# The state space kernels of eight channel groups on four column tiles of TensorE

## The chip, the cores and the metric

The kernel runs on one core of a Trainium2 chip. The metric is the device time of one execution in microseconds (us), taken as the median of several runs. Profiles come from one execution recorded by the hardware profiler. The engines are named as the profile names them: PE is TensorE (with PEld for its weight loads), ACT is ScalarE, DVE is VectorE, POOL is GpSimd, and SP is the engine whose queue issues most of the transfers.

## The reference: what is computed

One decoder block over 512 tokens and 16 meta tokens of width 1024, in float32: a half-weighted SwiGLU, then attention and a state space layer side by side, gated and merged, then a second half-weighted SwiGLU and a norm.

```python
h = h + 0.5 * swiglu(rmsnorm(h, ffn1_norm[i]), ffn1_w1[i], ffn1_w3[i], ffn1_w2[i])
hn = rmsnorm(h, mix_norm[i])
q, k, v, u, g_attn, g_ssm = jnp.split(hn @ w_in[i], SPLITS, axis=-1)
attn = sliding_window_attention(q, k, v, attn_sinks[i])
y = s5_ssm(u, ssm_a_re[i], ssm_a_im[i], ssm_log_step[i], ssm_b_re[i], ssm_b_im[i],
           ssm_c_re[i], ssm_c_im[i], ssm_d[i])
...
h = h + merged @ w_out[i]
h = h + 0.5 * swiglu(rmsnorm(h, ffn2_norm[i]), ffn2_w1[i], ffn2_w3[i], ffn2_w2[i])
return rmsnorm(h, final_norm)[:, N_META:]
```

The state space layer has 32 channel groups of 16 channels, each with 64 complex states. The kernel works on it in chunks of eight time steps. Within a chunk, the output of a group is its input times a small matrix that depends on the parameters alone: for each of the eight distances in time, a 16 by 16 block (input channel by output channel). The row of these blocks, 16 by 128 numbers for one group, is what the change is about. It is the product of a 128 by 16 matrix (the input matrix of the group, real and imaginary states below each other) and a 128 by 128 matrix (powers of the state's decay times the output matrix, for eight steps and 16 channels).

## The kernel before, in words

**The large products.** Nearly all of the time goes to products of weights with activations. Each float32 weight tile comes by an SP transfer into a tile `raw` (line 156). ACT rounds it to a high part `whi` (line 173), DVE forms the rest `wlo` (line 174), and PE multiplies high by high, high by low and low by high, all as float32r (line 238 for the first products of a SwiGLU, line 412 for its second ones, line 414 in the second SwiGLU). One output tile of 128 rows is a unit; in the first SwiGLU a unit of line 238 has 48 matmuls, since the 528 columns are taken as two halves of 264. Weights are prepared two units ahead of their use: while unit i is multiplied, the piece of unit i + 2 is prepared (`prep_piece`, called behind the unit's products in `step`), and three buffers of `whi` and `wlo` stand for it.

**The order of the work.** Instructions run on each engine in the order in which the program writes them (`manual_schedule`). The parameters of the state space layer are worked out beside the first SwiGLU, by a generator, `ssm_params`. In the loop over the units of the first SwiGLU (line 848), each unit from the fifth on takes one step of this generator, up to its next `yield`, and puts it between its matmuls, in the middle of the unit (the callables `mids`, cut in by `accumulate`). A step that holds matmuls thus interrupts a run of large matmuls on PE.

**The place of the change.** The last part of `ssm_params` (lines 636 to 673) handles the groups in four batches of eight. For a batch, POOL works out `Qt` (lines 639 to 642) and `Pb` (lines 644 to 648). Two steps later come the kernels. In one step, four matmuls (line 656) put the kernels of four groups side by side into one PSUM tile `psK`, 16 partitions by 512 columns, and ACT copies it to the tile `Kt` (line 658). In the next step the same follows for the other four groups, with another PSUM tile. Then POOL adds the direct term on `Kt` (line 663) and issues eight transfers that spread it over the matrix `Mt` (line 666), and two further steps transpose `Pb` on PE (four transposes each, line 671) with an ACT copy to `Wt` (line 672). `Mt`, `Qt` and `Wt` are read much later, in the mixing stage (lines 943, 992 and 993). The PSUM tiles of the generator come from a pool of four buffers of one bank each, `ps_ax`.

These matmuls are float32, not float32r. The profile records two LDWEIGHTS and two MATMULs for each of them: 64 of each for 32 matmuls. Their left operand has 16 columns, so only 16 columns of the array yield output.

Of the kernel before, what the change touches and what calls it, by code (L numbers as in the profile page):

```python
# [8 lines left out]
F32 = mybir.dt.float32  # L9
# [36 lines left out]
GB = 8  # L46
# [19 lines left out]
def hybrid_block_kernel(  # L66
# [47 lines left out]
    def bcol(b):  # L114
        return (b // 2) * HALF + (b % 2) * 128

# [1 line left out]
    ident = const.tile([128, 128], F32, name="ident")  # L118
    ones = const.tile([128, 128], F32, name="ones")
    gT = const.tile([128, 32], F32, name="gT")  # L120
# [3 lines left out]
    mhalf = const.tile([128, 6], F32, name="mhalf")  # L124
    st = const.tile([128, 6], F32, name="st")

# [1 line left out]
    raws = []  # L128
    pieces = []

# [68 lines left out]
            flush()  # L199

    def step2(ua, ub, mids=()):
        """Two units of which the last tile of operands comes late: it goes last in both."""
        a, b = ua[0](*take(), None), ub[0](*take(), None)
        next(a)
        for m in mids:
            m()
        prep_piece()
        next(b)
        for g in (a, b):
            for _ in g:  # L210
                pass
        ua[1]()
        prep_piece()
        ub[1]()
# [6 lines left out]
        return r  # L221

    def accumulate(seq, emit, mids):
        """One accumulation group; the callables in mids go out between its matmuls."""
        cuts = {len(seq) * (j + 1) // (len(mids) + 1): m for j, m in enumerate(mids)}
        for n, args in enumerate(seq):
            if n in cuts:
                cuts[n]()
            emit(*args, n == 0, n == len(seq) - 1)
# [24 lines left out]
        else:  # L254
            mm3([(ps, lambda r, k: real(r[:, k, :]))], hi, lo, rhi, rlo, nk, mids, k0)

# [1 line left out]
    def ffn_plan(w1, w3, w2, chunks, head=0, tail=False):  # L258
        f0 = 0
        for ci, n in enumerate(chunks):  # L260
# [39 lines left out]
        both(add_raw(ND, 256, wsrc(w_out[0], 0, ND, d * 128, 256)))  # L300
    ffn_plan(ffn2_w1[0], ffn2_w3[0], ffn2_w2[0], CHUNKS2, tail=True)

# [1 line left out]
    def new_hg(cols=COLS, p=hg_p):  # L304
        hi = p.tile([128, ND, cols], F32R, tag="hgh", name="hgh")
        lo = p.tile([128, ND, cols], F32R, tag="hgl", name="hgl")
# [40 lines left out]
        V.tensor_copy(st[:, 0:4], ps[:, 0:4])  # L347
        return st

# [1 line left out]
    def ffn_units(hg, hT, n528, mm_ps, g_p, t_p, chunks, last_hook=None, first_mm=None, tail=False):  # L351
        """The units of one half-residual SwiGLU, hT += 0.5 * its output; with tail, the last chunk's
        down projection is left out and its operands are returned."""
        w = HALF if n528 else 256
        units = []

# [92 lines left out]
                units.append(down(gs, n, d, last_hook if last else None))  # L449
        return units, gs  # L450

# [1 line left out]
    persist = ExitStack()  # L453
    tabs = ExitStack()
    tab = {}
# [16 lines left out]
    def ssm_params(ps_p):  # L472
# [111 lines left out]
        PE.transpose(ps[:16, 256:288], dn, ident[:NG, :NG])  # L584
        V.tensor_copy(T7.rearrange("p q g -> p (q g)"), ps[:, 0:224])
        V.tensor_copy(dT, ps[:16, 256:288])
        # the even groups' rows stay on the lower partitions, the odd ones' on the upper
        for i, (dst, q) in enumerate(((c8[:, 0, :], 2), (c8[:, 1, :], 3), (m8, 4))):
            v = T7[:, q, :].rearrange("p (j e) -> p j e", e=2)
            G.tensor_copy(dst[0:64], v[0:64, :, 0])  # L590
# [45 lines left out]
        for b in range(NB):  # L636
            gsl = slice(GB * b, GB * b + GB)
            tq = pp.tile([128, GB, T + 1, 16], F32, tag="s4", name="tq", bufs=2)
            G.tensor_tensor(out=Qt[:, gsl], in0=lam(LR, b, T + 1), in1=vec(A, 0, b, T + 1), op=ALU.mult)
            G.tensor_tensor(out=tq, in0=lam(LI, b, T + 1), in1=vec(A, 1, b, T + 1), op=ALU.mult)  # L640
            yield
            G.tensor_tensor(out=Qt[:, gsl], in0=Qt[:, gsl], in1=tq, op=ALU.add)
            Pb = pp.tile([128, GB, T, 16], F32, tag="s4", name="Pb", bufs=2)
            G.tensor_tensor(out=Pb, in0=lam(LR, b, T), in1=vec(BB, 0, b, T), op=ALU.mult)
            yield
            tq = pp.tile([128, GB, T, 16], F32, tag="s4", name="tq", bufs=2)
            G.tensor_tensor(out=tq, in0=lam(LI, b, T), in1=vec(BB, 1, b, T), op=ALU.mult)
            G.tensor_tensor(out=Pb, in0=Pb, in1=tq, op=ALU.add)
            yield
            yield  # L650
            Kt = pp.tile([16, GB, T, 16], F32, tag="s4", name="Kt", bufs=2)
            for h in range(2):
                ps = ps_p.tile([128, 512], F32, tag="ax", name="psK")
                for i in range(4):
                    g = GB * b + 4 * h + i
                    PE.matmul(out=ps[:16, 128 * i:128 * i + 128], lhsT=BB[:, 0, g, :],  # L656
                              rhs=Qt[:, g, 0:T, :].rearrange("p t c -> p (t c)"), start=True, stop=True)
                S.activation(out=Kt[:, 4 * h:4 * h + 4].rearrange("p g t c -> p (g t c)"), in_=ps[:16, :], func=AF.Copy)
                yield
            dg = pp.tile([16, GB, 16], F32, tag="dg", name="dg")  # L660
            G.tensor_tensor(out=dg, in0=ident[:16, 0:16].unsqueeze(1).to_broadcast([16, GB, 16]),
                            in1=dT[:, gsl].unsqueeze(2).to_broadcast([16, GB, 16]), op=ALU.mult)
            G.tensor_tensor(out=Kt[:, :, 0, :], in0=Kt[:, :, 0, :], in1=dg, op=ALU.add)
            for s in range(T):
                r0 = 16 * (T - 1 - s)
                G.dma_start(out=Mt[r0:r0 + 16, gsl, 16 * s:128],
                            in_=Kt[:, :, 0:T - s, :].rearrange("p g t c -> p g (t c)"))
            for h in range(2):
                ps = ps_p.tile([128, 512], F32, tag="ax", name="psW")
                for i in range(4):  # L670
                    PE.transpose(ps[:, 128 * i:128 * i + 128], Pb[:, 4 * h + i].rearrange("p t c -> p (t c)"), ident)
                S.activation(out=Wt[:, GB * b + 4 * h:GB * b + 4 * h + 4, :].rearrange("p g c -> p (g c)"), in_=ps, func=AF.Copy)
                yield
# [19 lines left out]
                n += w  # L693
            yield

# [1 line left out]
    G.memset(ones, 1.0)  # L697
    G.memset(ident, 0.0)
    G.affine_select(out=ident, in_=ident, compare_op=ALU.not_equal, fill=1.0, base=0, pattern=[[-1, 128]], channel_multiplier=1)
# [30 lines left out]
        S.dma_start(out=xm[h], in_=meta_tokens[8 * h:8 * h + 8, :])  # L730
    G.dma_start(out=srow, in_=attn_sinks)
    S.activation(out=rcol[:, 0:1], in_=mhalf[:, 0:1], func=AF.Silu)
    # the tensor engine's clock rises while the first loads are under way
    ps = ax_ps.tile([128, 512], F32, tag="ax", name="ps_w")
    for _ in range(WARM):
        PE.matmul(out=ps[:, 0:128], lhsT=ones, rhs=ones, start=True, stop=True)
# [22 lines left out]
        S.activation(out=hg[0][:, d, o], in_=hT[:, d, o], func=AF.Copy, scale=gT[:, d:d + 1])  # L759

    def x_in(h, d):
        """Block columns d of token half h: the transpose, then the two parts one and two blocks later."""
        if d < ND:
            x_t(h, d)
        if 0 <= d - 1 < ND:
            x_hi(h, d - 1)
        if 0 <= d - 2 < ND:
            x_lo(h, d - 2)
# [6 lines left out]
    firsts = []  # L775

    def first_mm(p, hi, lo, mids):
        """The first two units take the first half of the tokens first, while the second is brought in."""
        firsts.append((p, hi, lo))
        u = len(firsts) - 1  # L780
        for i, h in [(0, 0)] if u == 0 else [(1, 0), (0, 1), (1, 1)]:
# [82 lines left out]
    sf.close()  # L864
    hg = hg2

# [1 line left out]
    hd = tc.dram_tile([128, ND, COLS], F32, name="h_keep")  # L868
    G.dma_start(out=hd, in_=hT)
    sres.close()  # L870
# [24 lines left out]
    ud = tc.dram_tile([NB, 128, T, NCH], F32, name="u_steps")  # L895

    def ev_u(b):
        """Step-major u: [channel, (step, chunk)], the two chunks of meta tokens first; by way of DRAM
        it comes back as [(7 - step, channel of the group), (group, chunk)]."""
        def f(p):  # L900
            t = s_p.tile([128, T, NCH], F32, tag="uT", name="uT", bufs=2)

# [151 lines left out]
    tabs.close()  # L1054
    persist.close()

# [1 line left out]
    ps1.close()  # L1058
    ps3 = ExitStack()
    mm_ps = pool("ps_mm3", 3, space=PSUM, c=ps3)  # L1060
# [21 lines left out]
        G.tensor_copy(vr[m], vT[m][:, :, 256:264].unsqueeze(1).to_broadcast([128, 8, 2, 8]))  # L1082

    vmeta(0)
    # masks, with the sign that the negated scores need
    for t, m0, p0 in ((mA, 0, 16), (mC, 128, 0)):
        G.memset(t, 0.0)
        G.affine_select(out=t[:, p0:p0 + 128], in_=t[:, p0:p0 + 128], compare_op=ALU.is_gt, fill=1e30, base=0,
                        pattern=[[1, 128]], channel_multiplier=-1)
        G.affine_select(out=t[:, 144:272], in_=t[:, 144:272], compare_op=ALU.is_ge, fill=1e30, base=0,  # L1090
                        pattern=[[-1, 128]], channel_multiplier=1)
    # hm[p, h]: 1 where row p of the stacked meta probabilities belongs to head h
    V.tensor_reduce(out=hm, in_=ident.rearrange("p (l h k) -> p h l k", l=2, h=4), axis=mybir.AxisListType.XY, op=ALU.add)

    def ksplit(m):
# [73 lines left out]
        att[n] = (E, pm, [])  # L1169

    def s2(n, c, kb):
        """One block of keys: the probabilities' transpose."""
        E, _, tiles = att[n][:3]
        ps = pt_ps.tile([128, 512], F32, tag="pt", name="ps_t")
        for h in range(4):
            PE.transpose(ps[:, 128 * h:128 * h + 128], E[:, h, c:c + 128], ident)
        ph = a_p.tile([128, 512], F32R, tag="ph", name="ph", bufs=2)
        pl = a_p.tile([128, 512], F32R, tag="pl", name="pl", bufs=2)
        S.activation(out=ph, in_=ps, func=AF.Copy)
        V.tensor_tensor(out=pl, in0=ps, in1=fr(ph), op=ALU.subtract)  # L1180
        tiles.append((ph, pl, kb))
# [123 lines left out]

        step(*u, mids=[lambda fs=fs: [f() for f in fs] for fs in cuts], prep=False, hold=i < len(units) - 1)

# [1 line left out]
    at.close()  # L1309
    ps3.close()  # L1310
    kv.close()
# [46 lines left out]
            bcast_r(ax_ps, dgs[0], SEQ)  # L1358
    ps4.close()

    # the last chunk's down projection by halves of the tokens, each half's norm behind the products
    ps5 = ExitStack()
    mm_ps = pool("ps_mm5", 3, space=PSUM, c=ps5)
    z_ps = pool("ps_z", 2, space=PSUM, c=ps5)
# [112 lines left out]
```

## Time and profile before

| what | value |
|---|---|
| median of three runs | 1161.07 us (1159.37 to 1162.34) |
| span of the profiled execution, first to last instruction | 1160.7 us |
| granted TensorE clock of that execution, mean | 0.991 |
| PE busy | 1141.6 us, 98% of the span |
| PE weight loads busy | 1016.8 us, 88% |
| DVE / ACT / POOL busy | 632.1 / 410.4 / 361.5 us |
| first and last matmul of line 656 | 140.7 and 295.9 us from the span's start |

The profiled execution's own time is its span, 1160.7 us; the median of the runs is 0.4 us above it, which is what may lie around the span. A timeline row gives the start of a piece of work in us from the span's start, its length, the engine, the line, what is written from what, the shapes, and how many instructions were merged into the row. Matmuls are pipelined and the record of one is longer than the step from one to the next, so steps are read from starts, not from lengths.

### The profile page before, as it was taken

The numbers are of one execution on the slowest core, as the hardware profiler recorded it, in microseconds if no ns is written. First come the engines' busy times: TensorE is split into PE (matmuls) and PEld (weight loads), VectorE is DVE, ScalarE is ACT, GpSimd is POOL, SyncE is SP. The second block draws the span as 40 slices with busy tenths as digits, with TensorE's granted clock in tenths as the row PEclk, the third lists the DMA queues.
The fourth block names the chain that finished last, engine by engine and source line by source line (L and its number), as shares of the span: only waits on it lengthen the run. The fifth ranks groups of instructions, "written<-read, shape, count | busy, mean of one in ns | idle before, by whom it ended". The sixth has DMA issues, their size and how long they took to land.

```text
span 1160.7 us, 17253 instructions
## 1 busy us (share of the span) xinstructions
PE 1141.6 (98%) x7022; PEld 1016.8 (88%) x7022; DVE 632.1 (54%) x956; ACT 410.4 (35%) x719; POOL 361.5 (31%) x488
## 2 busy tenths in 40 slices
PE   9999999999999999999999999999999999999997
PEld 7999999999999999987778778878888888888887
DVE  5446653645444363767776777564544444444454
ACT  5322232232222242446565464353322222232234
POOL 1966662543685030425454331021000000000003
PEclk7999999999999999999999999999999999999999
DMA  5533233322423246121122222432333223323221
GB/s 158 115 96 109 73 92 94 91 84 83 110 74 101 69 144 191 48 73 60 51 73 73 73 68 79 145 109 73 108 109 110 73 82 103 112 86 117 84 73 73
DMA packets 105582, 108.42 MB, mean 93 GB/s; under 512 B 7504, under 2 KB 101968, under 8 KB 105376
## 3 DMA queue, kind: packets, MB, share of 16 engines
q1 hardware_dynamic: 103104, 100.74, 27.8%
q0 software_dynamic: 2352, 6.52, 2.2%
q8 instruction: 55, 0.90, 0.3%
q14 instruction: 23, 0.19, 0.1%
q10 hardware_dynamic: 48, 0.07, 0.0%
HBM read 100.80 MB, written 5.34 MB: 91 GB/s over the span
## 4 chain that ended last, share of the span: by engine, by line
PE 88%; DVE 4%; ACT 3%; POOL 2%; issue 2%; DMA 1%; POOLq 0%; DVEq 0%; SPq 0%; ACTq 0%
PE p L238 58%; PE p L412 11%; PE p L414 8%; PE p L798 2%; PE p L1372 1%; DMA hT<-h_keep 1%; ACT E L1157 1%; POOL m L1200 1%; POOL E L1168 1%; PE psK L656 1%; PE psY L992 1%; DVE wlo L174 1%; PE ps_x L744 1%; PE psY L993 1%; PE psS L943 1%
## 5 line engine op out<-in xcount | busy, mean ns | idle before, releaser
L238 PE MATMUL p<-hgh,whi 128*128 128x264 f32 (+1 forms) x1408 | 403.4, 333 | 0.1
L238 PE MATMUL p<-hgl,whi 128*128 128x264 f32 (+1 forms) x1408 | 402.4, 332 | 0.0
L238 PE MATMUL p<-hgh,wlo 128*128 128x264 f32 (+1 forms) x1408 | 400.9, 331 | 0.5 <-DVE wlo L174 0.5
L174 DVE TENSOR_TENSOR wlo<-raw,whi 128x1024 fp32r<-128x1024 f32 (+2 forms) x192 | 254.0, 1323 | 104.5 <-ACT whi L173 102.2
L238 PEld LDWEIGHTS p<-hgh,whi 128*128 128x128 f32 x1408 | 238.5, 188 | 26.0 <-issue 1.5
L238 PEld LDWEIGHTS p<-hgh,wlo 128*128 128x128 f32 x1408 | 238.2, 188 | 24.6 <-DVE wlo L174 1.0
L238 PEld LDWEIGHTS p<-hgl,whi 128*128 128x128 f32 x1408 | 238.4, 188 | 22.4
L173 ACT ACTIVATE whi<-raw 128x1024 fp32r<-128x1024 f32 (+2 forms) x192 | 187.5, 979 | 133.1 <-PE p L414 72.2
L1388 POOL TENSOR_TENSOR acc<-acc,zq 128x256 f32<-128x256 f32 x12 | 8.9, 738 | 349.8 <-ACT zq L1381 349.7
L384 ACT ACTIVATE t<-t 128x528 f32<-128x528 f32 (+1 forms) x44 | 28.1, 639 | 164.3 <-DVE t L383 164.3
L394 ACT ACTIVATE gh<-t 128x528 fp32r<-128x528 f32 (+1 forms) x44 | 28.1, 639 | 159.2 <-DVE t L393 159.2
L432 DVE SCALAR_TENSOR_TENSOR hT<-p,hT 128x528 f32<-128x528 f32 (+1 forms) x56 | 39.1, 698 | 82.8 <-PE p L414 52.2
L412 PE MATMUL p<-gh,whi 128*128 128x264 f32 x352 | 72.8, 288 | 0.7 <-DVE hT L432 0.5
L412 PE MATMUL p<-gl,whi 128*128 128x264 f32 x352 | 71.5, 284 | 0.0
L412 PE MATMUL p<-gh,wlo 128*128 128x264 f32 x352 | 71.4, 284 | 0.0
L383 DVE TENSOR_TENSOR t<-p,r_bc 128x528 f32<-128x528 f32 (+1 forms) x44 | 30.7, 698 | 70.4 <-PE p L238 67.3
L393 DVE TENSOR_TENSOR t<-p,t 128x528 f32<-128x528 f32 (+1 forms) x44 | 30.7, 698 | 63.8 <-PE p L238 63.5
L412 PEld LDWEIGHTS p<-gh,whi 128*128 128x128 f32 x352 | 54.4, 188 | 2.3 <-issue 1.2
L414 PE MATMUL p<-gh,whi 128*128 128x512 f32 x144 | 56.0, 389 | 0.0
L414 PE MATMUL p<-gl,whi 128*128 128x512 f32 x144 | 56.0, 389 | 0.0
L414 PE MATMUL p<-gh,wlo 128*128 128x512 f32 x144 | 56.0, 389 | 0.0
L412 PEld LDWEIGHTS p<-gl,whi 128*128 128x128 f32 x352 | 54.6, 188 | 0.0
(322 smaller groups left out, 1516.1 us busy)
## 6 DMA issues: line engine op xcount, KB each, us to landing
raw<-in_ffn_w_dram SPq DMA_DIRECT2D x42, 1024.0 KB, 5.4
raw<-in_ffn_w_dram SPq DMA_DIRECT2D x24, 768.0 KB, 4.3
raw<-in_w_in_dram SPq DMA_DIRECT2D x16, 1024.0 KB, 5.5
raw<-in_ffn_w_dram SPq DMA_DIRECT2D x12, 512.0 KB, 3.5
raw<-in_w_out_dram SPq DMA_DIRECT2D x4, 1024.0 KB, 8.7
h_keep<-hT POOLq DMA_DIRECT2D x1, 2112.0 KB, 7.3
raw<-in_ssm_glu_a_dram SPq DMA_DIRECT2D x4, 512.0 KB, 3.6
raw<-in_ssm_glu_b_dram SPq DMA_DIRECT2D x4, 512.0 KB, 4.6
```

The source lines that it names most:

```text
L173: S.activation(out=hi, in_=src, func=AF.Copy)
L174: V.tensor_tensor(out=lo, in0=src, in1=fr(hi), op=ALU.subtract)
L238: PE.matmul(out=o, lhsT=w[:, k0 + k, :], rhs=sl(r, k), start=start, stop=stop)
L383: V.tensor_tensor(out=t1, in0=cell[1], in1=rb(), op=ALU.mult)
L384: S.activation(out=t1, in_=t1, func=AF.Silu)
L393: V.tensor_tensor(out=t3, in0=cell[3], in1=cell["t1"], op=ALU.mult)
L394: S.activation(out=gh, in_=t3, func=AF.Copy)
L412: PE.matmul(out=p[:, h, :HALF], lhsT=wt[:, k, :], rhs=gs[k][c][:, h, :], start=start, stop=stop)
L414: PE.matmul(out=p, lhsT=wt[:, k, :], rhs=gs[k][c].rearrange("p h c -> p (h c)"), start=start, stop=stop)
L432: V.scalar_tensor_tensor(out=hv(hT, d), in0=cell["p"], scalar=0.5, in1=hv(hT, d), op0=ALU.mult, op1=ALU.add)
L656: PE.matmul(out=ps[:16, 128 * i:128 * i + 128], lhsT=BB[:, 0, g, :], rhs=Qt[:, g, 0:T, :].rearrange("p t c -> p (t c)"), start=True, stop= ...
L798: PE.matmul(out=p[:, h, :HALF], lhsT=w[:, k, :], rhs=r[:, k, h * HALF:(h + 1) * HALF], start=(n == 0), stop=(n == 3 * ND - 1))
```

## The change

For each batch of eight groups there is now one tile `psK` instead of two. The eight matmuls are written one behind the other, in two rounds of four. In a round, the four matmuls go to the four column tiles of the array, at columns 0, 32, 64 and 96 (`tile_position`), and so to partitions 0, 32, 64 and 96 of the PSUM tile; the second round takes the columns 128 to 255 of the PSUM tile. Column tile j holds the groups 2j and 2j + 1. ACT then makes four copies of 16 by 256 in place of two of 16 by 512, each from another quarter of the partitions to the same 16 partitions of `Kt`. The first two copies stand in the step of the eight matmuls, the other two in the next step, which has no matmul any more. The number of steps is the same. The rest of the file differs in comments and docstrings only; line numbers from 660 on rise by two.

```diff
             Kt = pp.tile([16, GB, T, 16], F32, tag="s4", name="Kt", bufs=2)
-            for h in range(2):
-                ps = ps_p.tile([128, 512], F32, tag="ax", name="psK")
-                for i in range(4):
-                    g = GB * b + 4 * h + i
-                    PE.matmul(out=ps[:16, 128 * i:128 * i + 128], lhsT=BB[:, 0, g, :],
-                              rhs=Qt[:, g, 0:T, :].rearrange("p t c -> p (t c)"), start=True, stop=True)
-                S.activation(out=Kt[:, 4 * h:4 * h + 4].rearrange("p g t c -> p (g t c)"), in_=ps[:16, :], func=AF.Copy)
-                yield
+            ps = ps_p.tile([128, 512], F32, tag="ax", name="psK")
+            for i in range(2):
+                for j in range(4):
+                    g = GB * b + 2 * j + i
+                    PE.matmul(out=ps[32 * j:32 * j + 16, 128 * i:128 * i + 128], lhsT=BB[:, 0, g, :],
+                              rhs=Qt[:, g, 0:T, :].rearrange("p t c -> p (t c)"), start=True, stop=True, tile_position=(0, 32 * j), skip_group_check=True)
+            for j in range(4):
+                S.activation(out=Kt[:, 2 * j:2 * j + 2].rearrange("p g t c -> p (g t c)"), in_=ps[32 * j:32 * j + 16, 0:256], func=AF.Copy)
+                if j % 2:
+                    yield
```

On PE, in the middle of the unit that takes the first of the two steps of the first batch, stand the following rows before the change (`p` is the unit's product, `hgh` and `hgl` the two parts of the activations):

```order
L238 MATMUL p<-hgl,whi 128x264 x2
L238 MATMUL p<-hgh,wlo 128x264 x2
L656 MATMUL psK<-Qt,BB 16x128 x4
L238 MATMUL p<-hgh,whi 128x264 x2
L238 MATMUL p<-hgl,whi 128x264 x2
```

At the same place after the change:

```order
L238 MATMUL p<-hgl,whi 128x264 x2
L238 MATMUL p<-hgh,wlo 128x264 x2
L656 MATMUL psK<-Qt,BB 16x128 x8
L238 MATMUL p<-hgh,whi 128x264 x2
L238 MATMUL p<-hgl,whi 128x264 x2
```

The eight matmuls of the batch now interrupt one unit; the middle of the next unit, where the other four stood, has none. The same holds for the other three batches.

On ACT, from the unit before the two steps to the one behind them, stand before the change (`t` and `gh` are tiles of the SwiGLU's evaluation):

```order
L384 ACTIVATE t_1610<-t_1610 128x528
L658 ACTIVATE Kt<-psK 16x512
L173 ACTIVATE whi<-raw 128x1024
L394 ACTIVATE gh<-t_1676 128x528
L658 ACTIVATE Kt<-psK 16x512
L173 ACTIVATE whi<-raw 128x1024
L384 ACTIVATE t_1741<-t_1741 128x528
```

And after it:

```order
L384 ACTIVATE t_1610<-t_1610 128x528
L659 ACTIVATE Kt<-psK 16x256 x2
L173 ACTIVATE whi<-raw 128x1024
L394 ACTIVATE gh<-t_1681 128x528
L659 ACTIVATE Kt<-psK 16x256 x2
L173 ACTIVATE whi<-raw 128x1024
L384 ACTIVATE t_1742<-t_1742 128x528
```

Each copy became two of half the columns, and nothing else moved on ACT.

## The prediction

> **What bounds the kernel now.** I read the page first: busy times and the chain of waits.
>
> ```profile
> span 1160.7 us, 17253 instructions
> PE 1141.6 (98%) x7022; PEld 1016.8 (88%) x7022; DVE 632.1 (54%) x956; ACT 410.4 (35%) x719; POOL 361.5 (31%) x488
> PE 88%; DVE 4%; ACT 3%; POOL 2%; issue 2%; DMA 1%; POOLq 0%; DVEq 0%; SPq 0%; ACTq 0%
> PE p L238 58%; PE p L412 11%; PE p L414 8%; PE p L798 2%; PE p L1372 1%; DMA hT<-h_keep 1%; ACT E L1157 1%; POOL m L1200 1%; POOL E L1168 1%; PE psK L656 1%; PE psY L992 1%; DVE wlo L174 1%; PE ps_x L744 1%; PE psY L993 1%; PE psS L943 1%
> ```
>
> PE is busy nearly throughout, and the chain that ends last runs over it; the kernels of the state space layer, line 656, are rounded to 1% of that chain, something like 10 us. A share of the whole program can hide a stage with another limit, so next comes the busy time in the stretch in which these matmuls lie (columns: window, its length, busy time and count on PE, PEld, DVE, ACT, POOL, then granted clock, DMA share, GB/s), and who made PE wait for weights.
>
> ```profile
> 140.00:310.00 170.00, 169.66 (x1379) 165.89 (x1378) 84.88 (x79) 47.03 (x64) 77.54 (x84) 1.00 0.31 88
> PE p L238 <- DVE wlo L174: 0.5, 1, 0.5
> ```
>
> In these 170 us PE is idle for 0.3 us, at the full clock, and every other engine is idle for at least half of the time. In the whole program PE waited once, for 0.5 us, for a weight part at line 238. So here a microsecond of PE is a microsecond of the kernel: what PE saves moves everything behind it forward.
>
> The third view is the chain in order of time, for the first and last of the eight bursts of line 656 (the eight rows are alike, 0.98 us each), and the tile's own rows.
>
> ```profile
> 140.77 0.98 PE psK L656 x8
> ...
> 295.18 0.98 PE psK L656 x8
> L656 PEld LDWEIGHTS psK<-Qt,BB x64: 92/97/97, 140.7 to 295.8; 128*16 128x16 f32 x64
> L656 PE MATMUL psK<-Qt,BB x64: 272/273/283, 140.7 to 295.9; 128*16 128x128 f32 x64
> ```
>
> A matmul is 273 ns from start to end, but a burst of eight instructions takes about 1 us: they overlap. What a burst really costs must be read from the timeline, around it.
>
> ```profile
> 139.63 0.41 PE L238 MATMUL p<-hgh,wlo 128*128 128x264 f32 x2
> ...
> 140.37 0.40 PE L238 MATMUL p<-hgh,wlo 128*128 128x264 f32 x2
> 140.70 1.05 PE L656 MATMUL psK<-Qt,BB 128*16 128x128 f32 x8
> 141.68 0.52 PE L238 MATMUL p<-hgh,whi 128*128 128x264 f32 x2
> 142.03 0.41 PE L238 MATMUL p<-hgl,whi 128*128 128x264 f32 x2
> ```
>
> Between 139.63 and 140.37 three pairs of large matmuls start: 0.74 / 3, some 0.245 us for a pair. From 140.37 to 142.03 are 1.66 us, in which two pairs go out (0.49 us). The burst costs the rest, **1.17 us**. Within it, the row's 1.05 us are seven steps and one whole matmul of 0.27 us, so one step is 0.78 / 7 = **0.11 us**. Eight steps are 0.88 us; the other **0.29 us** are a fixed cost of each burst. Is it the cost of any interruption? The transposes of line 671 answer that, full-width work cut into the same kind of run:
>
> ```profile
> 154.43 0.41 PE L238 MATMUL p<-hgh,wlo 128*128 128x264 f32 x2
> 154.67 0.60 PE L671 MATMUL psW<-ident,Pb 128*128 128x128 f32 x4
> 155.02 0.49 PE L238 MATMUL p<-hgh,whi 128*128 128x264 f32 x2
> 155.35 0.40 PE L238 MATMUL p<-hgl,whi 128*128 128x264 f32 x2
> ```
>
> From 154.43 to 155.35 are 0.92 us, less 0.49 for the two pairs: 0.43 us, which is four steps of 0.11 and nothing more. So the 0.29 us go with the narrow output: PE pays them for leaving the full array and coming back. The Trainium skill has this in "TensorEngine Tiling (Array Packing)", Key Properties: changing the tiling mode, not just the tile, drains the engine. The trace agrees, at 0.29 us for both changes.
>
> **The change part by part.** Before, a batch is two bursts, 2.34 us of PE; four batches are 9.4 us.
>
> *One interruption fewer per batch.* Eight matmuls now stand in one run between large ones, so the way out of the full array and back is paid once: 0.29 us less per batch, 1.2 us in all. This holds whatever else happens, unless changing the column tile costs something itself.
>
> *The 16 instructions on four column tiles.* No work in the trace of before goes to any column tile but the first, so it can't show whether tiles work side by side. The bounds are rows from above. At worst but for a penalty, the 16 go one behind the other, 16 x 0.11 = 1.76 us. At best, four tiles stream at once and the run is 4 x 0.11 = 0.44 us. Between the two decides the order of the two passes of a float32 matmul. The state space output later in the program, a narrow float32 product, shows it:
>
> ```profile
> 475.62 0.43 PE L992 MATMUL psY<-Mt,U 128*64 128x128 f32 x2
> 475.89 0.38 PE L993 MATMUL psY<-Qt,X 128*64 128x128 f32 x2
> 476.11 0.38 PE L992 MATMUL psY<-Mt,U 128*64 128x128 f32 x2
> ```
>
> The program writes one matmul of line 992, then one of line 993, and so on; PE gets each as two instructions in a row. So in the changed run the order is tile 0 twice, tile 1 twice, tile 2 twice. The two passes of one matmul use one tile and one output and can't go together. If PE starts instructions in order, the first pass on tile 1 can go beside the second pass on tile 0, but not sooner. Then the run is one step for the first pass, seven steps in which a second pass and the next matmul's first pass share the array, and one step for the last: 9 x 0.11 = 0.99 us. I take this value, between the two bounds, because of the rows of lines 992 and 993: tiles overlap, and the order that these rows show limits it to pairs. With the fixed 0.29 us a batch costs 1.28 us in place of 2.34: 1.06 us less, **4.2 us** in four batches.
>
> On the order, the Trainium skill says in "TensorE: Matmul & The Clock Gate", Part 3, that matmuls keep program order in start and in end. By this rule pairs are the most that can overlap, and the sum stays at 4.2 us; no row here shows it for several tiles.
>
> *ACT.* Half-size copies from PSUM are in the trace, of the same number of columns:
>
> ```profile
> L658 ACT ACTIVATE Kt<-psK 16x512 f32<-16x512 f32 x8 | 4.7, 589 | 28.2 <-PE psK L656 28.2
> L1113 ACT ACTIVATE VB<-ps_v 128x256 fp32r<-128x256 f32 x4 | 1.5, 379 | 0.1
>   POOL Kt L663: 81.9, 4
> L666 POOL DMA_DIRECT2D Mt<-Kt x32: 522/531/643, 150.3 to 301.4; - x32
> ```
>
> Two copies at 0.38 us take 0.76 in place of 0.59: 0.17 us more in each step, 1.4 us over the eight. In the first step of a batch they also start about 0.1 us later, since the run (1.28) is longer than a burst (1.17). Queued behind them on ACT is `whi` of line 173, then DVE's `wlo`, for a weight that PE uses two units on; a unit is 48 large matmuls, nearly 6 us. A delay of 0.3 us has that cover and costs nothing; bare, it would be 0.3 us at most for each of four units, 1.2 us. In the second step ACT no longer waits for PE at all, so its work there comes earlier. The copies end earlier for POOL too, which waited 81.9 us for them in four times, some 20 us each (the third row). Its eight transfers per batch keep their order on POOL's queue and are not short of time: the last is issued at 301.4 us (the fourth row), and `Mt`, which they fill, is first read at 475.62 us (the row of line 992). One PSUM tile fewer per batch leaves the pool's other uses as free as they were. All this at zero.
>
> The sum against the profiled span: 1160.7 - 4.2 = 1156.5 us; the median of the runs lies 0.4 above the span, so 1161.07 - 4.2 = **1156.9 us**, 0.36% less. What is late next is PE itself, with the large matmuls.
>
> **The rivals.**
>
> *No overlap.* The 16 instructions take their 1.76 us whatever the tile, 2.05 us per batch; only the saved interruption is left: 4 x 0.29 = 1.2 us, 1159.9 us. For it: float32 passes already take twice the steps per column of the float32r ones (128 columns in 0.11 us against 264 in 0.12), so something on the way in could be full. Against: with 16 of 128 columns in use, the array has the room.
>
> *Full overlap.* The passes of a matmul are issued, but tiles run ahead of each other, and four stream at once: 0.29 + 0.44 = 0.73 us per batch, 1.61 saved, 6.4 us in all, 1154.7 us. Against it: the pairs in the rows of line 992 and 993 come strictly in program order. The Trainium skill speaks for it in the same Part 3, with 2.38 times the speed for three column tiles; an estimate from 2.38 / 3 on four tiles would give 16 x 0.11 / 3.2 + 0.29 = 0.84 us and 6.0 us saved.
>
> *Changing the tile costs.* Seven of the 16 instructions go to another column tile than the one before. If each such change empties the array, or its weight load can't be hidden, the run gets longer than two bursts. The gain of 0.29 us is gone at 0.29 / 7 = 0.04 us per change; that is the point from which this rival makes the kernel slower. Prices from rows: a bare weight load, 0.097 us, added to the 2.05 us of the case without overlap gives 2.05 + 0.68 = 2.73 us against 2.34, 1.6 us slower; an emptied array, 0.273 - 0.11 = 0.16 us, gives 2.05 + 1.14 = 3.2 us, 0.85 more per batch, **3.4 us slower, 1164.5 us**; the whole 0.29 us of a mode change at each gives 7 us, 1168.1 us. For it: a change of mode is shown to cost that. Against: in the burst of before, weight loads of 0.097 us are wholly hidden in steps of 0.11, though all go to the same tile. The Trainium skill says, in that Part 3, that a weight load overlaps a running matmul only when the row group differs; the 0.11 us step, with one row group throughout, already speaks against taking this strictly.
>
> **How the numbers follow.** Pairs overlap (1156.9 us) 0.45; no overlap (1159.9) 0.25; full overlap (1154.7) 0.18; a tile change that costs (1162.6 to 1168.1) 0.12. About 0.3%, 3.5 us, is what a measurement of this kernel can tell from no change. The likeliest case lies 0.7 us beyond it, and the three runs spread over 3 us, so I count 0.32 of its 0.45 as faster; with full overlap that is 0.49. The rest of it, no overlap, and the cheap end of the tile change make 0.43 for within 0.3%; 0.08 is left for slower. The range takes in the first three cases with a microsecond around them, 1153.9 to 1161.0 us; left out are the costly tile change and the edges, somewhat under 0.2.
>
> **What the profile after would show.** Four bursts of line 656 with 16 instructions each, not eight with eight. Read as above, from the last large pair before a burst to the second after it, less 0.49 us: 1.28 us if pairs overlap, 2.05 if nothing does, 0.73 for full overlap, 2.7 or more if changing the tile costs. Within a burst, starts would come in pairs of nearly the same time, 0.11 us apart, in the first case, evenly 0.11 us apart in the second, in fours in the third. The middle of the following unit shows no interruption. ACT's copies should be near 0.38 us, eight per half. I would be wrong in the step "the gain passes through" if the burst shrinks as told but PE waits longer for `wlo` at line 238 or for `gh` at line 412 behind it.

## The result, and the profile after

The changed kernel takes 1155.44 us (median of five runs, 1154.81 to 1156.95), the kernel before 1162.07 us (median of five runs, the three of the table ahead of the prediction among them). The two medians are 6.6 us apart; the recorded ratio is 0.9949, with a 95% interval of 0.9936 to 0.9961, which is 5.9 us less, between 4.5 and 7.4, and so holds the 6.6 too. The forecast was 4.2 us less. It has the right sign and lies a little below this interval. The time itself, 1155.44, lies in the range, but that range was drawn wide enough for three different mechanisms, so it doesn't tell which of them is at work.

The page of the kernel after, the lines that were shown of before:

```profile
span 1154.1 us, 17264 instructions
PE 1135.5 (98%) x7022; PEld 1012.4 (88%) x7022; DVE 634.9 (55%) x956; ACT 411.6 (36%) x727; POOL 359.0 (31%) x488
PE 87%; DVE 4%; ACT 3%; POOL 2%; issue 2%; DMA 1%; SPq 0%; POOLq 0%; DVEq 0%; ACTq 0%
```

The stretch of the kernels, and the wait for weights at line 238:

```profile
140.00:310.00 170.00, 169.66 (x1430) 167.89 (x1430) 90.08 (x81) 49.41 (x73) 84.81 (x109) 1.00 0.32 95
```

```profile
PE p L238 <- DVE wlo L174: 0.2, 1, 0.2
```

PE does as many matmuls as before (7022) in 6 us less busy time, and is as full in the stretch as it was (idle 0.3 us of 170): more of its work fits into the same time, 1430 matmuls in place of 1379. No wait took the place of what went. Next, the timeline around the first batch, to be read as before the change:

```profile
140.58 0.40 PE L238 MATMUL p<-hgh,wlo 128*128 128x264 f32 x2
140.91 0.63 PE L656 MATMUL psK<-Qt,BB 128*16 128x128 f32 x16
141.47 0.51 PE L238 MATMUL p<-hgh,whi 128*128 128x264 f32 x2
141.82 0.41 PE L238 MATMUL p<-hgl,whi 128*128 128x264 f32 x2
```

From 140.58 to 141.82 are 1.24 us, less 0.49 for two pairs: **0.75 us** for a batch. Two bursts took 2.34. All four batches are alike, so 4 x 1.59 = 6.4 us went here, and the span fell by 1160.7 - 1154.1 = 6.6 us, at the same mean granted clock of 0.991. Nearly all of the gain is in this stage. How the 16 instructions share their 0.63 us is seen by ending the window a little later each time:

```profile
140.91 0.30 PE L656 MATMUL psK<-Qt,BB 128*16 128x128 f32 x4
140.91 0.41 PE L656 MATMUL psK<-Qt,BB 128*16 128x128 f32 x8
140.91 0.52 PE L656 MATMUL psK<-Qt,BB 128*16 128x128 f32 x12
```

The first four are done after 0.30 us, and one alone takes 0.28: they start within 0.02 us. Each further 0.11 us brings four more. Four steps, not nine: this is the rival "full overlap".

### The profile page after: what moved, and what is told of

It is laid out like the page before. It is cut to its first block, busy times and chain, and to the rows that moved or that the text cites. A ratio compares the mean times of both kernels' runs of the same rounds, so it can differ in the third digit from the quotient of the medians.

```text
span 1154.1 us, 17264 instructions
## 1 busy us (share of the span) xinstructions
PE 1135.5 (98%) x7022; PEld 1012.4 (88%) x7022; DVE 634.9 (55%) x956; ACT 411.6 (36%) x727; POOL 359.0 (31%) x488
## 4 chain that ended last, share of the span: by engine, by line
PE 87%; DVE 4%; ACT 3%; POOL 2%; issue 2%; DMA 1%; SPq 0%; POOLq 0%; DVEq 0%; ACTq 0%
PE p L238 58%; PE p L412 11%; PE p L414 8%; PE p L800 2%; ACT E L1159 1%; PE p L1374 1%; DMA hT<-h_keep 1%; POOL m L1202 1%; POOL E L1170 1%; DVE wlo L174 1%; PE psY L994 1%; PE psY L995 1%; PE psS L945 1%; PE ps_t L1178 1%; ACT whi L173 1%
## 5 line engine op out<-in xcount | busy, mean ns | idle before, releaser
L385 DVE TENSOR_TENSOR t<-t,r_bc 128x528 f32<-128x528 f32 (+1 forms) x44 | 37.2, 845 | 32.4 <-ACT t L384 32.4
```

What stands on the lines that cost most here:

```text
L385: V.tensor_tensor(out=t1, in0=t1, in1=rb(), op=ALU.mult)
```

## The experiments

Each kernel's batch is read off the timeline in the same way: from the last pair of large matmuls ahead of the run to the second pair behind it, less 0.49 us. The first batch is shown; in the chain of waits the four batches of a kernel have the same length. "Instruction" stands for one pass of a float32 matmul, with its own weight load; a matmul has two. The two kernels under "How far ahead" and the one under "The fixed cost" were executed once each, so only their batches are read and not their times.

**Theory and rivals after the result.** Four column tiles work at once, and the run takes as many steps of 0.11 us as the busiest tile has instructions, plus 0.29 us for leaving the full array and coming back. The rivals: the gain is that of the saved interruption or of the work that moves with it; or tiles do share the array, but PE starts instructions strictly in the order in which they reach it, and in the change the passes of a round's four matmuls happen to reach it interleaved (first pass of all four, then second pass of all four).

**One run on one tile.** All eight matmuls in one step, on the first column tile.

```diff
+            pk = []
             for h in range(2):
                 ps = ps_p.tile([128, 512], F32, tag="ax", name="psK")
+                pk.append(ps)
                 for i in range(4):
...
+            for h in range(2):
-                S.activation(out=Kt[...], in_=ps[:16, :], func=AF.Copy)
+                S.activation(out=Kt[...], in_=pk[h][:16, :], func=AF.Copy)
                 yield
```

> All eight matmuls of a batch stand in one step, as in the change, but all on the first column tile and in two PSUM tiles, with the two copies of before. Theory (four column tiles work at once, and the saved interruption is a side gain): 16 steps of 0.11 us and 0.29 us fixed, 2.05 us per batch in place of 2.34, so 1.2 us less than before, 0.1%. Rival (the gain is in the saved interruption, or in ACT's and POOL's work that moves with it): about 6 us less than before, as in the change.

The timeline of this kernel:

```profile
137.02 0.40 PE L238 MATMUL p<-hgh,wlo 128*128 128x264 f32 x2
137.36 1.92 PE L658 MATMUL psK<-Qt,BB 128*16 128x128 f32 x16
139.56 0.41 PE L238 MATMUL p<-hgl,whi 128*128 128x264 f32 x2
```

2.54 - 0.49 = 2.05 us per batch, 1.2 us less than before in four. The time is 0.9977 of before (0.9965 to 0.999), 1.2 to 4.1 us less. The interval's middle is above what the batches give; where the rest would be is not settled, but the 5.9 us of the change are outside it. The interruption is a minor part.

**Four tiles, two runs per batch.** The same number of interruptions as before.

```diff
-                for i in range(4):
-                    g = GB * b + 4 * h + i
-                    PE.matmul(out=ps[:16, 128 * i:128 * i + 128], ...)
-                S.activation(out=Kt[:, 4 * h:4 * h + 4]..., in_=ps[:16, :], func=AF.Copy)
+                for j in range(4):
+                    g = GB * b + 4 * h + j
+                    PE.matmul(out=ps[32 * j:32 * j + 16, 0:128], ..., tile_position=(0, 32 * j), skip_group_check=True)
+                for j in range(4):
+                    S.activation(out=Kt[:, 4 * h + j]..., in_=ps[32 * j:32 * j + 16, 0:128], func=AF.Copy)
                 yield
```

> Four column tiles, but four matmuls per step as before, so eight bursts of eight instructions, and one copy of 16 by 128 per group. Theory: two steps of 0.11 us and 0.29 us fixed, 0.51 us per burst in place of 1.17, so 5.3 us less than before. Rival (the saved interruption makes the gain): no change against before.

```profile
140.52 0.40 PE L238 MATMUL p<-hgh,wlo 128*128 128x264 f32 x2
140.86 0.41 PE L656 MATMUL psK<-Qt,BB 128*16 128x128 f32 x8
141.55 0.40 PE L238 MATMUL p<-hgl,whi 128*128 128x264 f32 x2
```

1.03 - 0.49 = 0.54 us per burst against 1.17, so 5.0 us in eight; the time is 0.9942 of before (0.9919 to 0.9965). The tiles alone make most of the gain.

**Two tiles.** The change on the columns 0 and 32 only.

```diff
-            for i in range(2):
-                for j in range(4):
-                    g = GB * b + 2 * j + i
+            for i in range(4):
+                for j in range(2):
+                    g = GB * b + 4 * j + i
...
-            for j in range(4):
-                S.activation(out=Kt[:, 2 * j:2 * j + 2]..., in_=ps[32 * j:32 * j + 16, 0:256], func=AF.Copy)
-                if j % 2:
-                    yield
+            for j in range(2):
+                S.activation(out=Kt[:, 4 * j:4 * j + 4]..., in_=ps[32 * j:32 * j + 16, :], func=AF.Copy)
+                yield
```

> As the change, but on two column tiles, at columns 0 and 32, with four matmuls for each and two copies of 16 by 512. Theory: eight steps of 0.11 us with two starts each and 0.29 us fixed, 1.17 us per batch, 4.7 us less than before. Rival (in order, passes of a matmul one behind the other): the first start alone, then pairs, nine steps, 1.28 us per batch, 4.2 us less than before.

```profile
137.24 0.40 PE L238 MATMUL p<-hgh,wlo 128*128 128x264 f32 x2
137.58 1.05 PE L656 MATMUL psK<-Qt,BB 128*16 128x128 f32 x16
138.91 0.41 PE L238 MATMUL p<-hgl,whi 128*128 128x264 f32 x2
```

16 instructions in the 1.05 us that eight took on one tile; 1.67 - 0.49 = 1.18 us per batch, eight steps and not nine. The time, 0.9945 of before (0.9924 to 0.9966), doesn't tell 4.7 us from 4.2; the batch does.

**Tile by tile.** Does PE start in order, with the passes interleaved, or does each tile go its own way? The order of writing tells.

```diff
-            for i in range(2):
-                for j in range(4):
+            for j in range(4):
+                for i in range(2):
                     g = GB * b + 2 * j + i
+                    m = 16 + 4 * i + j
-                    PE.matmul(out=ps[32 * j:32 * j + 16, 128 * i:128 * i + 128], lhsT=BB[:, 0, g, :], ...)
+                    PE.matmul(out=ps[32 * j:32 * j + m, 128 * i:128 * i + 128],
+                              lhsT=BB.rearrange("p a g c -> p (a g c)")[:, 16 * g:16 * g + m], ...)
```

> As the change, but the eight matmuls are written tile by tile: both matmuls of the first tile, then both of the second, and so on, so that four instructions for one tile stand behind each other. The left operands are 16 to 23 columns wide (the added output rows are read by nobody), so that each record tells its matmul. Theory (tiles run on their own, an instruction waits only for its own tile): starts still come in fours, of four different tiles, four steps of 0.11 us, 0.75 us per batch, and the time of the change, 6.4 us less than before. Rival (PE starts instructions in the order written, and in the change the two passes of the four matmuls of a round were interleaved on their way to it): a tile's first pass can start only beside the last pass of the tile before, so 13 steps, 1.72 us per batch, 2.5 us less than before.

The timeline, the first four by themselves and then all 16:

```profile
140.92 0.40 PE L238 MATMUL p<-hgh,wlo 128*128 128x264 f32 x2
141.25 0.33 PE L657 MATMUL psK<-Qt,BB 128*16 128x128 f32 x4
141.25 0.65 PE L657 MATMUL psK<-Qt,BB 128*16 128x128 f32 x16
142.18 0.40 PE L238 MATMUL p<-hgl,whi 128*128 128x264 f32 x2
```

The same first four, by their shapes (128*16 is an operand of 16 columns, and so the first tile's):

```profile
L657 PE MATMUL psK<-Qt,BB x4: 283/284/286, 141.3 to 141.3; 128*16 128x128 f32 x1, 128*17 128x128 f32 x1, 128*18 128x128 f32 x1, 128*19 128x128 f32 x1
```

The first four to start are one each of the widths 16, 17, 18 and 19, the four tiles, though three more instructions of the same tile are written between any two of them. An instruction overtakes those written ahead of it when they are another tile's. So the order of writing, which the description of the kernel before gives as the order on each engine, is not the order of starts on PE across column tiles. 1.26 - 0.49 = 0.77 us per batch, and 0.9959 of before (0.9944 to 0.9973), 3.1 to 6.5 us less: the theory's 6.4 lies in it, the rival's 2.5 doesn't. In-order start is out.

One more thing is in these rows. The first four take 0.33 us here and 0.30 in the change, one alone 0.284: three starts in 0.045 us against three in 0.017, some 14 ns against 6. Four instructions stand from one tile's first to the next's here, two in the change. This fits a PE that hands them out in the order written, some 3 to 4 ns each, to tiles that then work through their own; two differences of a few nanoseconds don't show it yet.

**How far ahead.** If so, how many instructions does a tile take ahead, before those behind them in the program have to wait? Two tiles, written tile by tile, with 16 and with eight instructions of the first tile ahead of the second's. The first edit is shown against the kernel of two tiles (its operand widths, changed as in the run before, are left out), the second against the first.

```diff
-            for i in range(4):
-                for j in range(2):
+            for j in range(2):
+                for i in [*range(4), *range(4)]:
```

> Two column tiles, written tile by tile, and each matmul made twice (the second time onto the same output), so that 16 instructions for the first tile stand ahead of the first one for the second tile; operands 16 to 23 columns wide as labels. Theory (PE hands instructions out in order, about 3.3 ns each, and each tile works through its own): the second tile starts 16 x 3.3 = 53 ns after the first, 16 steps of 0.11 us with two starts each, 2.05 us per batch. Rival (PE sees only a few instructions ahead, enough for the four of the tile-by-tile run but not more): the second tile starts only when some 12 of the first tile's instructions are gone, 12 x 0.11 = 1.3 us later, and the batch takes about 3.4 us.

The timeline of the first batch:

```profile
136.19 0.40 PE L238 MATMUL p<-hgh,wlo 128*128 128x264 f32 x2
136.53 3.25 PE L657 MATMUL psK<-Qt,BB 128*16 128x128 f32 x32
140.06 0.41 PE L238 MATMUL p<-hgl,whi 128*128 128x264 f32 x2
```

What of line 657 had started before 137.84 and before 137.86 us (the second tile's operands are 20 columns wide and more; a row lists its four commonest shapes):

```profile
L657 PE MATMUL psK<-Qt,BB x12: 272/272/283, 136.5 to 137.7; 128*16 128x128 f32 x4, 128*17 128x128 f32 x4, 128*18 128x128 f32 x2, 128*19 128x128 f32 x2
...
L657 PE MATMUL psK<-Qt,BB x14: 272/273/287, 136.5 to 137.9; 128*16 128x128 f32 x4, 128*17 128x128 f32 x4, 128*18 128x128 f32 x3, 128*19 128x128 f32 x2
```

Here the theory as I had put it falls, and the rival's number holds: 3.87 - 0.49 = 3.38 us per batch. Before 137.84 us twelve instructions of the first tile have started and nothing else. Two more follow at once: the thirteenth of the first tile (the third of width 18) and one of none of the four widths listed, which hold 13 of the 14; its width is 20, so it is the second tile's first. This would follow if a tile takes four ahead, the running one among them, and the fifth, with all behind it in the program, waits. A look-ahead that all tiles share doesn't give it: in the tile-by-tile run twelve instructions stood ahead of the fourth tile's first, and it started within 0.05 us. The same with eight ahead:

```diff
-                for i in [*range(4), *range(4)]:
+                for i in range(4):
```

> Two column tiles, written tile by tile, each matmul made once, so that eight instructions for the first tile stand ahead of the second tile's first. Theory (a tile takes four instructions ahead, the one that runs among them, and holds up those behind it in the program beyond that): the second tile starts with the fifth instruction of the first, 4 x 0.11 = 0.45 us after its start; 12 steps of 0.11 us and 0.29 us fixed, 1.6 us per batch. Rival (the second tile comes at once when its instructions are few enough, and the 16 of the run before were too many for one common queue): both tiles start within 0.03 us, 1.18 us per batch.

```profile
140.46 0.40 PE L238 MATMUL p<-hgh,wlo 128*128 128x264 f32 x2
140.80 1.50 PE L657 MATMUL psK<-Qt,BB 128*16 128x128 f32 x16
142.58 0.41 PE L238 MATMUL p<-hgl,whi 128*128 128x264 f32 x2
```

What had started before 141.24 and before 141.26 us:

```profile
L657 PE MATMUL psK<-Qt,BB x4: 272/272/283, 140.8 to 141.1; 128*16 128x128 f32 x2, 128*17 128x128 f32 x2
...
L657 PE MATMUL psK<-Qt,BB x6: 272/273/287, 140.8 to 141.2; 128*16 128x128 f32 x2, 128*17 128x128 f32 x2, 128*18 128x128 f32 x1, 128*20 128x128 f32 x1
```

Up to 141.24 us four of the first tile have started; the next two, by 141.26, are its fifth (width 18) and the second tile's first (width 20), some 0.45 us after 140.80. The batch takes 2.12 - 0.49 = 1.63 us, 12 steps. Four ahead was the number before the run, and it holds. In the tile-by-tile run four was just what each tile got, which is why it lost nothing.

**The fixed cost.** One run on one tile, with an operand as wide as the array.

```diff
-                    PE.matmul(out=ps[:16, 128 * i:128 * i + 128], lhsT=BB[:, 0, g, :],
+                    PE.matmul(out=ps[:, 128 * i:128 * i + 128], lhsT=BB.rearrange("p a g c -> p (a g c)")[:, 16 * g:16 * g + 128],
```

> The run of eight matmuls on one tile, with a left operand of 128 columns in place of 16 (the operands of the groups behind it; the added output rows are read by nobody), so that the array need not leave its full width. Theory (the fixed 0.29 us are the way from the full array to a column tile and back): 16 steps of 0.11 us and nothing fixed, 1.79 us per batch. Rival (the fixed cost goes with float32 between float32r, or with the run itself): 2.05 us per batch as with 16 columns.

```profile
137.50 0.40 PE L238 MATMUL p<-hgh,wlo 128*128 128x264 f32 x2
137.74 1.95 PE L658 MATMUL psK<-Qt,BB 128*128 128x128 f32 x16
139.76 0.40 PE L238 MATMUL p<-hgl,whi 128*128 128x264 f32 x2
```

2.26 - 0.49 = 1.77 us, against 2.05 with 16 columns: 0.28 of the 0.29 us go with the narrow operand, not with the float32 or the interruption. "TensorEngine Tiling (Array Packing)" in the Trainium skill, Key Properties, has a drain at a change of tiling mode; if that is the cost, these two runs give its price. That PE drains is not seen in a trace by itself.

**ACT's copies twice.** The change, each copy made two times.

```diff
             for j in range(4):
-                S.activation(out=Kt[:, 2 * j:2 * j + 2]..., in_=ps[32 * j:32 * j + 16, 0:256], func=AF.Copy)
+                for _ in range(2):
+                    S.activation(out=Kt[:, 2 * j:2 * j + 2]..., in_=ps[32 * j:32 * j + 16, 0:256], func=AF.Copy)
```

> The change, with each of ACT's copies made twice (same source, same place), 0.38 us more for each, 1.5 us of ACT more per batch, 6 us in all. Theory (ACT's copies lie beside PE's work and cost nothing): the time of the change. Rival (weights are held up behind the copies): up to 6 us more than the change.

The copies' row, of the change and then of this kernel:

```profile
L659 ACT ACTIVATE Kt<-psK x16: 373/377/381, 141.7 to 288.1; 16x256 f32<-16x256 f32 x16
```

```profile
L660 ACT ACTIVATE Kt<-psK x32: 372/376/380, 141.3 to 288.5; 16x256 f32<-16x256 f32 x32
```

16 copies more of 0.376 us, 6.0 us of ACT, and the time is 1156.25 us beside 1156.65 us of the change, run again on the same chip: 0.9941 of before (0.9925 to 0.9958) against 0.9936 (0.9918 to 0.9954). The rival's 6 us would have brought it back to about the time of before; ACT's part is off the path.

> The change itself, beside the next three on the same chip: 0.76 us per batch in place of 2.35, about 6.4 us less than before.

That second measurement of the change, 0.9936, agrees with the first.

**The outputs too.** What eight groups gain in the kernels, the state space outputs should gain on two tiles of 64 columns. Here too each tile gets four instructions in a row, the number that it takes ahead.

```diff
-        for h in range(2):
-            ps = ax_ps.tile([128, 512], F32, tag="ax", name="psY")
-            for i in range(4):
+        ps = ax_ps.tile([128, 512], F32, tag="ax", name="psY")
+        for i in range(4):
+            for h in range(2):
                 g = GB * b + 4 * h + i
-                o = ps[:64, 128 * i:128 * i + 128]
+                o = ps[64 * h:64 * h + 64, 128 * i:128 * i + 128]
-                PE.matmul(out=o, lhsT=u[:, 4 * h + i, 2:NCH], rhs=Mt[:, g, :], start=True, stop=False)
+                PE.matmul(out=o, lhsT=u[:, 4 * h + i, 2:NCH], rhs=Mt[:, g, :], start=True, stop=False,
+                          tile_position=(0, 64 * h), skip_group_check=True)
...
+                          tile_position=(0, 64 * h), skip_group_check=True)
-            S.activation(out=y[:, :, 4 * h:4 * h + 4, :]..., in_=ps[:64, :]..., func=AF.Gelu_apprx_tanh)
+        for h in range(2):
+            S.activation(out=y[:, :, 4 * h:4 * h + 4, :]..., in_=ps[64 * h:64 * h + 64, :]..., func=AF.Gelu_apprx_tanh)
```

> The change, and the state space outputs in the same manner: their matmuls yield 64 rows, and those of the upper four groups of a batch go to the column tile at 64, so that a batch has one PSUM tile psY in place of two, with two copies from its two halves. Theory (two tiles of 64 columns work at once just as four of 32): 16 steps of 0.11 us in place of 32 per batch, 1.75 us less in each of four batches, 7 us less than the change. Rival (matmuls that add onto an open output, or 64 columns wide, don't share the array, or the later start of the first copy makes PE wait): no change against the change.

The first batch's outputs, from the large pair ahead to the second pair behind, in the change:

```profile
469.12 0.40 PE L238 MATMUL p<-hgh,wlo 128*128 128x264 f32 x2
469.46 0.43 PE L994 MATMUL psY<-Mt,U 128*64 128x128 f32 x2
...
473.45 0.41 PE L238 MATMUL p<-hgl,whi 128*128 128x264 f32 x2
```

And in this kernel:

```profile
469.19 0.40 PE L238 MATMUL p<-hgh,wlo 128*128 128x264 f32 x2
469.52 0.45 PE L994 MATMUL psY<-Mt,U 128*64 128x128 f32 x4
...
471.81 0.41 PE L238 MATMUL p<-hgl,whi 128*128 128x264 f32 x2
```

4.33 - 0.49 = 3.84 us became 2.62 - 0.49 = 2.13 us: 1.71 less per batch, 6.8 us in four. The time is 1150.12 us, 0.989 of before (0.9874 to 0.9905), beside 0.9936 of the change. This version beats both kernels, by some 12 us and some 6.

## Why the prediction was right in direction and short in size

*PE bounds the stretch, so what PE saves moves the end.* Right: 6.4 us less in the four batches, 6.6 us less in the span, and PE's wait for `wlo` at line 238 went from 0.5 to 0.2 us.

*The cost of a burst, 1.17 us, with 0.29 us fixed.* Right in size: 0.28 us is what separates 16 columns from the full width in the runs on one tile, and in the batches fewer interruptions alone give 1.2 us per kernel, as in the sum.

*The 16 instructions in nine steps.* This step failed: "If PE starts instructions in order, the first pass on tile 1 can go beside the second pass on tile 0, but not sooner." The premise was taken from the rows of lines 992 and 993, which show the order on one tile only and can't speak for several. In the runs a second pass that has to wait for its own tile doesn't hold up the next tile's first pass, as long as no tile has more than four ahead. Four steps and not nine: 0.75 us per batch in place of 1.28, which over four batches is the whole of the 2 us by which the sum fell short. The rival "full overlap", 0.73 us and 6.4 us, was the right case, and the prediction gave it a chance of 0.18. The rule of the Trainium skill that I had put beside this step, from "TensorE: Matmul & The Clock Gate", Part 3, that matmuls keep program order in start and end, doesn't hold across column tiles here: in the tile-by-tile run the fourth tile's first pass starts within 0.05 us of the first tile's, and three passes of the first tile written ahead of it start later. The measured speed of several column tiles in the same part, which I had left to the rival, was the better guide: its estimate was 0.84 us per batch, and 0.75 was measured.

*No overlap, and a tile change that costs.* Both are out: two tiles take half of the steps of one, and 16 instructions with a change of tile at nearly every second take no longer than the steps of the busiest tile. A line of the same Part 3 has weight loads overlap running matmuls only when the row group differs, though the text above it also lets a load into a background buffer go ahead; here all share one row group, and loads of 0.097 us are hidden in steps of 0.11.

*ACT and POOL at zero.* Right: the copies take 0.377 us, as estimated, and twice as many change nothing that the runs can tell.

*The time around the span.* The 0.4 us, ahead of the prediction and in its sum, were a mistake of small size: they compared the span of one execution with the median of others. The changed kernel's profiled execution has a span of 1154.1 us and a time of 1155.9, so 1.8 us lie around it. By luck this helped the forecast: the three runs of before that it started from had a median 1 us below that of the five. From 1162.07 the sum would have given 1157.9 us, 2.4 above the measured time in place of 1.5.

*Two slips of arithmetic.* 0.32 and 0.18 make 0.50 for faster, not 0.49, and a microsecond around the three cases is 1153.7 to 1160.9 us, not 1153.9 to 1161.0. Neither changes an answer.

## What to carry to other kernels

Where PE is full, look for matmuls whose output has 64 rows or fewer: put on several column tiles, they took the steps of the busiest tile here (16 rows on two and four tiles, 64 rows on two), in one PSUM tile. The copies followed their columns and not their partitions: 0.377 us for 16 by 256, where 128 by 256 took 0.379. Spread the tiles in the order of writing, so that no tile has more than four instructions (two float32 matmuls) in a row while others stand idle: the same 16 instructions took eight steps alternating and 12 tile by tile. And put such work together, since each interruption of full-width work by a narrow run cost some 0.3 us.

## What the runs showed of the hardware

- A matmul can start ahead of one written before it, on another column tile: written tile by tile, the first passes of four tiles start within 0.05 us. In the order of the change four start within 0.02 us.
- A column tile takes four instructions ahead, with the running one. With 16 of one tile ahead, the second tile began with the thirteenth; with eight, with the fifth; with four, at once.
- A matmul that adds onto an open output shares the array too: the outputs went from 3.84 to 2.13 us on two tiles of 64 columns.
- A run of 16-column float32 matmuls between full-width ones costs 0.29 us beside its steps (2.05 us for 16 instructions); the same run at full width costs its steps alone (1.77 us).
